# Preparing the right operands of a seven-product scheme earlier, value tiles by pairs of heads, and five pairs of input tiles instead of four

## The chip, the cores and the metric

The kernel runs on one core of a Trainium2 chip. The metric is the device time of one execution in microseconds (us). Less is better. Before the change three runs gave 1080.13, 1081.16 and 1081.58 us, a median of 1081.16 us.

## What is computed

One decoder layer over 1024 positions of width 1024, in float32. The part that the change touches is the first half of the layer, the mixer:

```
u = rms_norm(x, norm1_g)
z = u @ w_in                      # 1024 x 3584 columns
cb, cc, ch = three groups of 512 columns (convolution)
rq, rk, rv, rg = four groups of 512 columns (retention, 4 heads of 128)
y_conv = group_rms_norm(cb * causal_dwconv3(cc * ch))
q, k   = rotary(rq), rotary(rk);  v = rv
o      = chunkwise_retention(q, k, v)      # per head, 8 chunks of 128 rows
y_ret  = group_rms_norm(o) * silu(rg)
x = x + concat(y_conv, y_ret) @ w_out
```

Behind it stand an MLP with a squared ReLU (1024 to 4096 to 1024) and a last norm. The change doesn't touch those.

## The kernel before, in words

**Matrix products.** Everything is held transposed, channels on the partitions. Each float32 operand is split in two parts of a shorter format, hi and lo, and a product is taken as hi by hi, hi by lo and lo by hi. `split_piece` (L166) makes the two parts of a weight piece: `wh` by a copy on ACT, `wl = r - wh` by a subtraction on DVE, or on POOL where the planner's clock for POOL stands low enough. The input has the parts `uh` and `ul` for each of eight groups of 128 channels. The matmuls (all on L401, in `mm`) are 128x128 weights by 128x512 columns.

**A whole tile** is 128 columns of `z` for all 1024 positions. `tile_in` (L518) makes it in four quarters, two banks of PSUM at a time: 8 channel groups x 2 halves of positions x 3 products = 48 matmuls. `whole(f)` (L741) then takes it out of PSUM and starts the elementwise work of that tile, as convolution input or as gate.

**A pair** (`pair_in`, L821) makes two tiles of `z` at once with seven products of half the size in place of eight, in the manner of Strassen and Winograd: 7 products x 4 channel groups x 3 = 84 matmuls where two whole tiles take 96. Three of the seven have parts of `uh` and `ul` as their right operands, 36 matmuls; the other four need sums and differences of the input, called t1 to t4, 48 matmuls. These right operands are the tiles `U` (a hi and a lo part in one tile of 1024 columns). The generator `rights(j)` (L782) makes them for channel group j = 0 to 3: two DMAs that load the input anew into tiles `xs`, two scalings on ACT, four subtractions on DVE or POOL, then for each of t1 to t4 a copy on ACT (hi) and a subtraction on DVE or POOL (lo). Its first line waits for the end of a retention: `rights(0)` and `rights(1)` for that of the first, `rights(2)` and `rights(3)` for that of the second. Each pair also needs sums of weight pieces (`r<-r,r`, three per pair, on POOL) and sums of its products on DVE (`z<-z,b`, line 74).

**Retention.** `retention(p, q, k)` (L577) works on two heads, p = 0 or 1, in ten steps, one chunk of 128 positions after another: scores and transposes on PE, masks, states and tiny scale factors on DVE (`h<-b,bk,causal`, `S<-S,b`, and `m`, two columns wide), scaled copies on ACT. Its last PE instructions are the transposes on L661. The values are computed before it (L350 to L363) into four tiles `v` of 1024 columns, each with two chunks of all four heads.

**What sets the order of the work.** The program is written out by a planner in Python: `Task`s (generators) yield what they wait for, and `tick` and `background` put their next operations among the matmuls when the planner's own clocks of the engines say so. A group of 12 matmuls is one slot, 2.72 us on that clock. `IN_TURNS` (L40) is the order of the tiles after the four query and key tiles: a number is a whole tile, a bracket a pair. Before: whole tiles 0, 1, 2, 3 and 20, then the pairs (4,5), (6,7), (8,9) and (10,11), then 21; then come 22 and 23 (`IN_END`). Retention 1 runs among the first whole tiles. Tiles in SBUF of 128 x 1024 come from one pool, `big`, of 40 buffers. All elementwise operations are issued by one helper, so they have line 74 in the profile; they are told apart by the names of their tiles. After the mixer come the out-projection (L938 and on) and the MLP, L401 and L1274 by turns.

Of the kernel before, what the change touches and what calls it, by code (L numbers as in the profile page):

```python
# [16 lines left out]
P = 128  # L17
D = 1024
T = 1024
H = 512  # L20
# [16 lines left out]


IN_QK = [12, 13, 16, 17, 14, 15, 18, 19]
IN_TURNS = [0, 1, 2, 3, 20, (4, 5), (6, 7), (8, 9), (10, 11), 21]  # L40
IN_END = [22, 23]
SLOT, LOOK, PE_MARGIN, LATE = 2.72, 3.2, 1.2, 0.0
WARM = 10
# [36 lines left out]
def hybrid_layer(  # L80
# [41 lines left out]
    def unit(dt=F32, s="u"):  # L122
        return big.tile([P, T], dt, tag="u", name=nm(s))
# [217 lines left out]

    v = [unit(s="v") for _ in range(NC_ // 2)]
    rtok = cp.tile([P, NC_], F32, name="rtok")
    ms = xp.tile([P, NC_], F32, name="ms")
    r2 = xp.tile([P, NC_], F32, name="r2")
# [12 lines left out]
                        stop=(k == KT - 1 and a is ul),  # L360
                    )
    for c in range(NC_):
        act.copy(v[c // 2][:, hs[c % 2]], vb[c])  # L363

    def token_norms():
        b = bank(pr)
# [210 lines left out]
    def retention(p, q, k):  # L577
# [7 lines left out]
        for c in range(NC_ + 2):  # L585
            yield STEP_MARGIN
            now[0] += 1.7
            new = None
            if c < NC_:
                sl = slice(c * P, (c + 1) * P)  # L590
                bs = bank(pr)
                for j in range(2):
                    nc.tensor.matmul(bs[:, js[j]], k[j][:, sl], q[j][:, sl], start=True, stop=True)
                kz = None
                if c < NC_ - 1:
                    bt = bs[:, 2 * P :]
# [14 lines left out]
                new = (c, sc, kz)  # L611
                retention_task[p].ready = clock[dve]
            done, pend = pend, new
            turned, turn = turn, None
            if done is not None:
                pc, sc, kz = done
                psl = slice(pc * P, (pc + 1) * P)
                vt = v[pc // 2]
                v0 = (pc % 2) * H + h0 * P
                vj = [vt[:, v0 + j * P : v0 + (j + 1) * P] for j in range(2)]  # L620
                bo = bank(pr)
                for j in range(2):
                    nc.tensor.matmul(bo[:, js[j]], sc[:, js[j]], vj[j], start=True, stop=(S is None))
                    if S is not None:
                        nc.tensor.matmul(
                            bo[:, js[j]], q[j][:, psl], S[:, js[j]], start=False, stop=True
                        )
                if kz is not None:
                    bk = bo[:, 2 * P :]
                    for j in range(2):  # L630
                        nc.tensor.matmul(bk[:, js[j]], kz[:, js[j]], vj[j], start=True, stop=True)
# [24 lines left out]
                turn = (pc, on)  # L656
            if turned is not None:
                pc, on = turned
                b = bank(pr)
                for j in range(2):  # L660
                    nc.tensor.transpose(b[:, js[j]], on[:, js[j]], ident)  # L661
                for j in range(2):
                    act.copy(o[j][:, pc * P : (pc + 1) * P], b[:, js[j]])
                    if pc % 4 == 3:
                        o_n[h0 + j, pc // 4] = o[j]
                        mark(("o", h0 + j, pc // 4), act)
            if c >= NC_ - 1:
                retention_task[p].ready = clock[act]
            if c == NC_:
                mark(("retention", p), act)  # L670


# [78 lines left out]

        tile_in(evac)

    for p in range(2):
        q = rot_tiles(*ropes)
        if p == 0:
            rows_ = norm_rows()
        k = rot_tiles(*ropes)
        tick()
        spawn(retention(p, q, k), max(clock[dve], clock[pool]))  # L760
        retention_task[p] = procs[-1]
        del q, k


    U = {}

    def put_hi(name, j, src):
# [5 lines left out]
        hi, lo = U[name][j]  # L773
        eng.tensor_sub(lo, src, f32(hi))

    def product(n, bank_):
        name = {1: "11", 2: "21", 3: "22", 4: "t4", 5: "t1", 6: "t2", 7: "t3"}[n]
        b = bank(bank_)
        mm(parts.pop(0), [b], lambda _, k: U[name][k], True, True)
        return b  # L780

    def rights(j):  # L782

        yield "retention", j // 2
        if j % 2:
            yield "t4", j - 1
        a, b = (unit(s="xs") for _ in range(2))
        lo_, hi_ = hs
        for k, t in ((j, a), (4 + j, b)):
# [10 lines left out]
        eng.tensor_sub(b[:, hi_], b[:, hi_], a[:, lo_])  # L800
        eng = yield (pool, dve)
        eng.tensor_sub(b[:, lo_], b[:, lo_], b[:, hi_])
        for name, src in (("t1", a[:, lo_]), ("t2", b[:, hi_]), ("t3", a[:, hi_]), ("t4", b[:, lo_])):
            yield (act,)
            put_hi(name, j, src)
# [2 lines left out]
            mark((name, j), eng)  # L808

    rights_task = []  # L810
    for j in range(4):
        rights_task.append(Task(rights(j), now[0]))
        rights_task[j].go()
    spread_norms(rows_)
    for j in range(4):
        for c, name in ((0, "11"), (1, "21"), (2, "22")):
# [707 lines left out]
```

## Time and profile before

| | |
|---|---|
| three runs | 1080.13, 1081.16, 1081.58 us |
| the profiled execution, its time | 1082.14 us |
| the same, the span of its instructions | 1080.3 us |
| mean granted clock of TensorE | 0.995 |

Engines: PE is TensorE's matmuls, PEld its weight loads, DVE is VectorE, ACT ScalarE, POOL GpSimd, SP SyncE, whose queue issues the transfers. A row of the timeline has the start in us, the duration, engine, line, operation, the tiles it writes and reads, and in square brackets how long the engine stood idle before it and who released it. A row of a window table has the window, its length, the engine's busy time with its number of instructions (those cut by the ends count too), the granted clock as a share of full speed, then the share of the DMA engines and their GB/s. Matmuls overlap in the pipeline, so the duration of one is longer than the distance to the next.

### The profile page before, as it was taken

How to read it: one execution, taken by the hardware profiler on the slowest of the kernel's cores; microseconds unless marked ns; L12 is line 12 of the kernel's file. 1: busy time of each engine (PE TensorE's matmuls, PEld its weight loads, DVE VectorE, ACT ScalarE, POOL GpSimd, SP SyncE). 2: the span in 40 equal slices, each digit the busy share in tenths (PEclk: the TensorE clock that was granted, in tenths of full speed). 3: DMA queues.
4: the chain of work that ended last, by engine and by line, in shares of the span. 5: the costliest groups of instructions: out<-in, count | busy, mean ns of one | idle time of the engine just before them, and what ended most of it. 6: DMA issues, size and time to landing. Idle time of an engine off the chain costs nothing.

```text
span 1080.3 us, 14040 instructions
## 1 busy us (share of the span) xinstructions
PE 1060.6 (98%) x4936; PEld 882.7 (82%) x4936; DVE 881.2 (82%) x1255; ACT 463.3 (43%) x916; POOL 540.3 (50%) x370
## 2 busy tenths in 40 slices
PE   9999999999999999999999999999999999999996
PEld 7888888887778888788788888888888888888886
DVE  8446546799997666699999989999899899899945
ACT  8211445763335544444343443443343434334453
POOL 6233323256752132559548258267286295384543
PEclk9999999999999999999999999999999999999998
DMA  7121121212223635050121211211301211210204
GB/s 273 62 59 48 31 79 69 100 58 77 69 59 117 224 114 169 2 194 30 58 69 39 79 39 49 89 25 54 93 25 50 88 30 43 85 30 12 77 1 157
DMA packets 40311, 81.75 MB, mean 76 GB/s; under 512 B 4528, under 2 KB 6704, under 8 KB 40240
## 3 DMA queue, kind: packets, MB, share of 16 engines
q1 hardware_dynamic: 40240, 80.85, 23.2%
q8 instruction: 39, 0.64, 0.2%
q14 instruction: 32, 0.26, 0.1%
HBM read 71.40 MB, written 9.44 MB: 75 GB/s over the span
## 4 chain that ended last, share of the span: by engine, by line
PE 80%; DVE 11%; issue 3%; POOL 3%; ACT 2%; DMA 1%; POOLq 0%; DVEq 0%; SPq 0%; ACTq 0%
PE b L401 50%; PE b L1274 23%; PE b L355 4%; DVE z L74 2%; DVE wl L74 2%; POOL r L74 1%; POOL z L74 1%; DVE t L74 1%; DVE x L74 1%; DVE xs L74 1%; DVE U L74 1%; DVE q L74 1%; ACT h L74 1%; PE b L337 1%; DVE m L74 1%
## 5 line engine op out<-in xcount | busy, mean ns | idle before, releaser
L401 PE MATMUL b<-U,wh 128*128 128x512 f32 x1024 | 315.9, 390 | 2.4 <-DVE x L74 1.2
L74 ACT CAST wh<-r 128x512 fp32r<-128x512 f32 x286 | 175.9, 620 | 321.2 <-PE b L401 134.7
L74 DVE TENSOR_TENSOR wl<-r,wh 128x512 fp32r<-128x512 f32 x251 | 233.3, 932 | 90.9 <-ACT wh L74 90.0
L74 POOL TENSOR_TENSOR r<-r,r 128x512 f32<-128x512 f32 x136 | 209.8, 1545 | 116.0 <-DVE wl L74 65.6
L1274 PE MATMUL b<-V,wh 128*128 128x512 f32 x784 | 242.0, 389 | 0.7 <-POOL V L74 0.4
L401 PEld LDWEIGHTS b<-U,wh 128*128 128x128 f32 x1024 | 191.8, 188 | 43.4 <-issue 2.8
L74 DVE TENSOR_TENSOR x<-x,b 128x512 f32<-128x512 f32 (+1 forms) x320 | 197.8, 663 | 24.4 <-PE b L401 19.3
L401 PE MATMUL b<-U,wl 128*128 128x512 f32 x512 | 199.4, 389 | 0.0
L1274 PEld LDWEIGHTS b<-V,wh 128*128 128x128 f32 x784 | 147.0, 188 | 32.3 <-POOL V L74 0.8
L74 POOL TENSOR_TENSOR t<-t,t 128x512 f32<-128x512 f32 x70 | 106.3, 1523 | 97.9 <-ACT t L74 51.9
L1274 PE MATMUL b<-V,wl 128*128 128x512 f32 x392 | 152.5, 389 | 0.0
L74 POOL TENSOR_TENSOR wl<-r,wh 128x512 fp32r<-128x512 f32 x35 | 49.1, 1408 | 159.2 <-ACT wh L74 151.9
L401 PEld LDWEIGHTS b<-U,wl 128*128 128x128 f32 x512 | 96.0, 188 | 20.7 <-POOL wl L74 0.4
L401 PE MATMUL b<-uh,wh 128*128 128x512 f32 x304 | 103.3, 399 | 2.3 <-DVE z L74 2.3
L401 PE MATMUL b<-uh,wl 128*128 128x512 f32 x304 | 100.8, 392 | 1.1 <-DVE wl L74 1.1
L401 PE MATMUL b<-ul,wh 128*128 128x512 f32 x304 | 101.0, 392 | 0.0
L1274 PEld LDWEIGHTS b<-V,wl 128*128 128x128 f32 x392 | 73.6, 188 | 15.2
L74 POOL TENSOR_TENSOR V<-t,V 128x512 fp32r<-128x512 f32 x35 | 49.6, 1417 | 67.2 <-ACT V L74 67.2
L74 DVE TENSOR_TENSOR t<-t,b 128x512 f32<-128x512 f32 x112 | 75.8, 677 | 1.7 <-POOL t L74 1.2
L74 ACT ACTIVATE t<-t 128x512 f32<-128x512 f32 x64 | 40.2, 631 | 81.9 <-DVE t L74 81.3
L74 DVE TENSOR_TENSOR V<-t,V 128x512 fp32r<-128x512 f32 x63 | 70.3, 1116 | 0.0
L401 PEld LDWEIGHTS b<-uh,wl 128*128 128x128 f32 x304 | 57.3, 189 | 13.9 <-DVE wl L74 1.5
(168 smaller groups left out, 1431.0 us busy)
## 6 DMA issues: line engine op xcount, KB each, us to landing
r<-w_up_t SPq DMA_DIRECT2D x64, 256.0 KB, 2.6
r<-w_down_t SPq DMA_DIRECT2D x56, 256.0 KB, 2.7
r<-w_in_t SPq DMA_DIRECT2D x48, 256.0 KB, 2.6
xt<-xT SPq DMA_DIRECT2D x16, 256.0 KB, 5.4
xs<-xT SPq DMA_DIRECT2D x8, 512.0 KB, 4.8
r<-w_out_t SPq DMA_DIRECT2D x16, 256.0 KB, 2.7
x<-xT SPq DMA_DIRECT2D x8, 512.0 KB, 7.4
k<-x SPq DMA_DIRECT2D x6, 512.0 KB, 3.2
```

The lines of the kernel that those rows point to most:

```text
L74: return f(out, *args, **kw)
L337: nc.tensor.matmul(b[:, c * P : (c + 1) * P], d, ident, start=True, stop=True)
L355: nc.tensor.matmul(vb[i], a[k][:, i * P : (i + 1) * P], b[k // 2][:, vs], start=(k == 0 and a is uh and b is vh), stop=(k == KT - 1 and a ...
L401: nc.tensor.matmul(b, a[:, k, :], rhs(n, k)[r], start=(start and i == 0), stop=(stop and i == len(ops) - 1),)
L1274: nc.tensor.matmul(b, a, r, start=(i == 0), stop=(i == len(ops) - 1))
```

## The change

The values are kept by pairs of heads: `v[p, i]` holds four chunks of the two heads of retention p. The copies out of PSUM are 16 of 128x256, half on ACT and half on DVE, in place of 8 of 128x512 on ACT, and the two tiles of p are given back when retention p ends. `rights(j)` no longer waits for whole retentions at its start: its loads and first four subtractions go as soon as the first queries and keys are there (j = 0), or t4 of j = 0 (j = 1), the second queries and keys (j = 2), or t4 of j = 2 (j = 3); the waits for retention 0, t4 of j = 1 and retention 1 stand ahead of the second part of j = 1, 2 and 3. The order of the tiles is 20, 0, 1, then five pairs from (2,3) to (10,11), then 21. The order of the weight transfers follows `IN_TURNS`.

```
-IN_TURNS = [0, 1, 2, 3, 20, (4, 5), (6, 7), (8, 9), (10, 11), 21]
+IN_TURNS = [20, 0, 1, (2, 3), (4, 5), (6, 7), (8, 9), (10, 11), 21]
...
-    v = [unit(s="v") for _ in range(NC_ // 2)]
+    v = {(p, i): unit(s="v") for p in range(2) for i in range(2)}
...
     for c in range(NC_):
-        act.copy(v[c // 2][:, hs[c % 2]], vb[c])
+        for p, eng in ((0, act.copy), (1, dve.tensor_copy)):
+            to = slice(c % 4 * 2 * P, (c % 4 + 1) * 2 * P)
+            eng(v[p, c // 4][:, to], vb[c][:, p * 2 * P : (p + 1) * 2 * P])
...
             if c == NC_:
+                for i in range(2):
+                    del v[p, i]
                 mark(("retention", p), act)
...
     def rights(j):
-        yield "retention", j // 2
-        if j % 2:
-            yield "t4", j - 1
+        yield [("qk", 0), ("t4", 0), ("qk", 1), ("t4", 2)][j]
         a, b = (unit(s="xs") for _ in range(2))
...
         eng.tensor_sub(b[:, lo_], b[:, lo_], b[:, hi_])
+        if j:
+            yield [("retention", 0), ("t4", 1), ("retention", 1)][j - 1]
         for name, src in (("t1", a[:, lo_]), ("t2", b[:, hi_]), ("t3", a[:, hi_]), ("t4", b[:, lo_])):
...
+        mark(("qk", p), dve)
+        if p == 0:
+            for j in range(4):
+                rights_task.append(Task(rights(j), now[0]))
+                rights_task[j].go()
```

The whole program has 12 matmuls of 128x512 fewer on PE: those with `U` as the right operand go from 1024 to 1056 (`wh`) and from 512 to 528 (`wl`), the three kinds with `uh` or `ul` from 304 to 284 each. DVE has 14 instructions more, POOL 8 more (four sums of weight pieces and five splits `wl` more, one other less), ACT 3 more, SP as many as before.

Three places show how the order moves. The first is PE at the end of retention 1, whose last transposes are the row with L661; before:

```order
L401 MATMUL b_1803<-uh_164,wl_1529 128x512
L661 MATMUL b_1983<-ident,h_1934 128x128 x2
L401 MATMUL b_2004<-uh_157,wh_1641 128x512
L401 MATMUL b_2005<-uh_157,wh_1641 128x512
L401 MATMUL b_2004<-ul_165,wh_1641 128x512
L401 MATMUL b_2005<-ul_165,wh_1641 128x512
L401 MATMUL b_2004<-uh_157,wl_1642 128x512
```

After, where the line numbers are two higher:

```order
L403 MATMUL b_1858<-uh_164,wl_1581 128x512
L663 MATMUL b_2023<-ident,h_1980 128x128 x2
L403 MATMUL b_2047<-uh_157,wh_1694 128x512
L403 MATMUL b_2047<-ul_165,wh_1694 128x512
L403 MATMUL b_2047<-uh_157,wl_1695 128x512
L403 MATMUL b_2047<-uh_158,wh_1694 128x512
L403 MATMUL b_2047<-ul_166,wh_1694 128x512
```

Before, a whole tile follows (two banks by turns, b_2004 and b_2005), and one more after it, and then the first pair; after, the first product of the first pair (one bank) follows at once. The transposes are the 872nd row of PE's order in both.

The second place is DVE within retention 0. `m` are the tiny scale factors, `h` the masked scores, `S` the state; before:

```order
L74 SCALAR_TENSOR_TENSOR m_998<-m_998 128x2
L74 SCALAR_TENSOR_TENSOR h_1033<-b_1028,bk,causal 128x128 x2
L74 SCALAR_TENSOR_TENSOR S_1046<-S_990,b_1039 128x128 x2
L74 SCALAR_TENSOR_TENSOR m_1050<-m_1050,bq 128x2
L74 TENSOR_TENSOR m_1054<-m_1054 128x2
L74 SCALAR_TENSOR_TENSOR m_1054<-m_1054,m_1050 128x2
L74 SCALAR_TENSOR_TENSOR m_1054<-m_1054 128x2
L74 SCALAR_TENSOR_TENSOR h_1083<-b_1078,bk,causal 128x128 x2
```

After:

```order
L74 SCALAR_TENSOR_TENSOR m_966<-m_966 128x2
L74 TENSOR_TENSOR U_993<-xs_872,U_993 128x512
L74 TENSOR_TENSOR U_996<-xs_871,U_996 128x512
L74 SCALAR_TENSOR_TENSOR h_1022<-b_1017,bk,causal 128x128 x2
L74 SCALAR_TENSOR_TENSOR S_1035<-S_959,b_1028 128x128 x2
L74 SCALAR_TENSOR_TENSOR m_1039<-m_1039,bq 128x2
L74 TENSOR_TENSOR m_1043<-m_1043 128x2
L74 SCALAR_TENSOR_TENSOR m_1043<-m_1043,m_1039 128x2
L74 SCALAR_TENSOR_TENSOR m_1043<-m_1043 128x2
L74 TENSOR_TENSOR U_1055<-xs_872,U_1055 128x512
```

The lo parts of right operands (`U<-xs,U`) now stand between the chunk steps of retention 0.

The third place is DVE towards the end of the pair (4,5), which is the first pair before and the second after. `wl` is the lo part of a weight piece, `z` and `cv` are sums of products and convolution values; before:

```order
L74 TENSOR_TENSOR wl_2350<-r_2189,wh_2349 128x512
L74 TENSOR_TENSOR z_2200<-z_2200,b_2336 128x512
L74 SCALAR_TENSOR_TENSOR cv_2250<-a_2095,sm,cv_2250 128x512 x2
L74 TENSOR_TENSOR wl_2376<-r_2218,wh_2375 128x512
L74 TENSOR_TENSOR z_2200<-z_2200,cv_2250 128x512
L74 TENSOR_TENSOR wl_2402<-r_2245,wh_2401 128x512
L74 TENSOR_TENSOR z_2360<-z_2361,b_2388 128x512
```

After:

```order
L74 TENSOR_TENSOR wl_2371<-r_2210,wh_2370 128x512
L74 TENSOR_TENSOR z_2216<-z_2216,b_2357 128x512
L74 SCALAR_TENSOR_TENSOR cv_2259<-z_2046,sm,cv_2259 128x512 x2
L74 TENSOR_TENSOR wl_2396<-r_2234,wh_2395 128x512
L74 TENSOR_TENSOR z_2216<-z_2216,cv_2259 128x512 x2
L74 TENSOR_TENSOR z_2380<-z_2381,b_2409 128x512
```

Of two neighbours one has changed: the last split `wl` of the piece stands on POOL after the change, and a product `z<-z,cv` on DVE that stood on POOL. From `z_2360` (before) and `z_2380` (after) to the end of the program DVE has the same 957 rows in both, and PE, ACT and POOL have the same rows too, from 240.8, 270.5 and 268.2 us of the profile of before on.

More of the change, by code (lines that the diff above doesn't have):

```diff
@@ L617, in retention @@
                 psl = slice(pc * P, (pc + 1) * P)
-                vt = v[pc // 2]
-                v0 = (pc % 2) * H + h0 * P
+                vt = v[p, pc // 4]
+                v0 = pc % 4 * 2 * P
                 vj = [vt[:, v0 + j * P : v0 + (j + 1) * P] for j in range(2)]
@@ L752, in whole @@
         tile_in(evac)
[L754 to L762, printed above, removed]
     U = {}
@@ L774, in put_lo @@
         eng.tensor_sub(lo, src, f32(hi))
[L776 to L780, printed above, removed]
     def rights(j):
-        yield "retention", j // 2
-        if j % 2:
-            yield "t4", j - 1
+        yield [("qk", 0), ("t4", 0), ("qk", 1), ("t4", 2)][j]
         a, b = (unit(s="xs") for _ in range(2))
@@ L810, in hybrid_layer, with product @@
     rights_task = []
-    for j in range(4):
-        rights_task.append(Task(rights(j), now[0]))
-        rights_task[j].go()
+    for p in range(2):
+        q = rot_tiles(*ropes)
+        if p == 0:
+            rows_ = norm_rows()
+        k = rot_tiles(*ropes)
+        tick()
+        spawn(retention(p, q, k), max(clock[dve], clock[pool]))
+        retention_task[p] = procs[-1]
+        del q, k
+        mark(("qk", p), dve)
+        if p == 0:
+            for j in range(4):
+                rights_task.append(Task(rights(j), now[0]))
+                rights_task[j].go()
+    def product(n, bank_):
+        name = {1: "11", 2: "21", 3: "22", 4: "t4", 5: "t1", 6: "t2", 7: "t3"}[n]
+        b = bank(bank_)
+        mm(parts.pop(0), [b], lambda _, k: U[name][k], True, True)
+        return b
     spread_norms(rows_)
```

## The prediction

> **What bounds the kernel now.** I read the page first, then PE's waits in the stretch from 210 to 330 us, then the windows of that stretch, and last DVE's timeline there. The shares and the slices of the page:
>
> ```profile
> PE 1060.6 (98%) x4936; PEld 882.7 (82%) x4936; DVE 881.2 (82%) x1255; ACT 463.3 (43%) x916; POOL 540.3 (50%) x370
> ...
> DVE  8446546799997666699999989999899899899945
> ```
>
> PE is busy 98% of the span, so a removed matmul should count in full, unless PE then waits. DVE's slices (27 us each) are at nine tenths from the eighth to the eleventh, about 190 to 300 us: there the pairs of input tiles run. How the two stages differ:
>
> ```profile
> 100.00:210.00 110.00, 108.80 (x634) 94.39 (x633) 68.42 (x171) 54.76 (x201) 33.22 (x25) 1.00 0.18 61
> 210.00:320.00 110.00, 104.88 (x450) 84.19 (x450) 104.27 (x111) 52.83 (x89) 66.85 (x43) 0.99 0.23 75
> ```
>
> The columns behind the length are PE, PEld, DVE, ACT, POOL. From 100 to 210 us (queries, keys, retentions, first whole tiles) PE is idle 1.2 us and DVE is busy 62%. From 210 to 320 us PE is idle 5.1 us and DVE is busy 95%. PE's waits in that second stretch, and three of them on the timeline:
>
> ```profile
> PE b L401 <- DVE z L74: 2.3, 1, 2.3
> PE b L401 <- DVE wl L74: 1.1, 1, 1.1
> PE b L481 <- ACT s L74: 1.0, 1, 1.0
> PE b L482 <- DVE s L74: 0.4, 2, 0.2
> PE b L482 <- DVE r L74: 0.3, 1, 0.3
> 264.82 0.50 PE L401 MATMUL b<-uh,wl 128*128 128x512 f32 x1 [1.12 <-DVE wl L74]
> 268.65 0.50 PE L482 MATMUL b<-s,blkr 128*128 128x512 f32 x1 [0.22 <-DVE s L74]
> 318.60 0.80 PE L401 MATMUL b<-uh,wh 128*128 128x512 f32 x1 [2.27 <-DVE z L74]
> ```
>
> They add up to the idle time, and nearly all of it is DVE's doing. So in the pair stage two engines are close to being the bound: PE leads, catches up with DVE and waits. The change takes matmuls from PE and adds work to DVE in just this stage, and the wait at 264.82 us decides what it is worth.
>
> After the longest wait the clock falls:
>
> ```profile
> 319.00:320.00 1.00, 1.00 (x3) 0.50 0.00 0
> 321.00:322.00 1.00, 1.00 (x4) 0.57 0.00 0
> 322.00:323.00 1.00, 1.00 (x6) 1.00 0.00 0
> 318.60 12.48 PE b L401 x47
> 331.98 108.81 PE b L401 x480
> ```
>
> The next to last number of a window's main columns is the granted clock (0.50, 0.57, 1.00). The last two rows are of the chain: 480 matmuls take 108.81 us where PE runs freely, 0.2267 us each; the 47 behind the wait take 12.48 us in place of 10.65, so the slow clock cost 1.8 us.
>
> **The change part by part.** *Matmuls.* 12 fewer x 0.2267 = 2.72 us. Both orders reach the end of retention 1 at the same row of PE, at 209.8 us of before:
>
> ```profile
> 209.79 0.52 PE L661 MATMUL b<-ident,h 128*128 128x128 f32 x2
> 210.07 0.71 PE L401 MATMUL b<-uh,wh 128*128 128x512 f32 x2
> ```
>
> From there PE alone would come to the matmul that waits for `wl` 2.72 us sooner: it stood ready at 264.82 - 1.12 = 263.70 us, and would at 260.98 us.
>
> *DVE and POOL from there to that split.* Before, the first pair began when the two whole tiles behind retention 1 were through, and DVE issued 26 instructions from its first row of that pair (at 238.13 us) to the split's end at 264.77 us. After, two pairs lie between retention 1 and the same split, and in the order I count 50 DVE instructions from the first row of pair (2,3) through the split, beside 21 on POOL. Prices from the same stage:
>
> ```profile
> 238.13:264.77 26.64, 24.30 (x28) 1.00 0.24 70
> 212.59:264.70 52.11, 49.36 (x52) 1.00 0.24 81
> 264.80:323.70 58.90, 55.19 (x60) 0.97 0.22 67
> 212.59:264.70 52.11, 32.47 (x21) 1.00 0.24 81
> 263.01 1.76 DVE L74 TENSOR_TENSOR wl<-r,wh 128x512 fp32r<-128x512 f32 x1
> ```
>
> The first three are DVE's windows (each counts two that its ends cut), the fourth is POOL's for the second. The last pair-sized piece costs 26.64 / 26 = 1.025 us per DVE instruction, gaps included; the 50 whole ones from 212.59 us cost 52.11 / 50 = 1.042, and those also run beside 21 POOL instructions; the next 60, up to the long wait, cost 58.90 / 60 = 0.982. When can DVE begin?
>
> ```profile
> 210.80 0.69 DVE L74 TENSOR_TENSOR U<-xs,U 128x512 fp32r<-128x512 f32 x1
> 211.41 1.28 DVE L74 TENSOR_TENSOR z<-b,R 128x512 f32<-128x512 f32 x2
> ```
>
> At the end of retention 1 DVE is not behind: it takes a whole tile's product out of PSUM at 211.41 us, directly after PE has finished it. I let the pair's work begin at 211.7 us, an estimate from these two rows. Then the split is done at 211.7 + 50 x 1.025 = 262.95 us, against 264.77 us: 1.8 us sooner. PE, ready at 260.98 us, waits 2.0 us in place of 1.12 us and goes on 0.05 us behind the split as before, at 263.0 us, 1.8 us sooner. At 0.982 it is done at 260.8 us, PE doesn't wait and is 3.84 us ahead there; at 1.042, at 263.8 us, 1.0 us ahead. It would be no gain at 1.061. I take 1.025, because that row has the kinds of instruction that the second of the new pairs has, and no subtractions for the right operands.
>
> *After that.* From there to the end all engines have the same rows. The waits of 1.00, 0.22, 0.27 and 2.27 us are between instructions of that common part, and the DVE lag that ends in the wait at 318.60 us builds up again from 264.80 us on, where DVE has been waited out. So they come again, and the shift stays -1.8 us to the end.
>
> *Right operands made early.* The loads of `xs`, 8 of 512 KB, now stand on SP's queue inside retention 0 and 1, with weight pieces behind them.
>
> ```profile
> xs<-xT SPq DMA_DIRECT2D x8, 512.0 KB, 4.8
> 194.75 0.97 DVE L74 TENSOR_TENSOR m<-m 128x2 f32<-128x2 f32 x1 [0.27 <-ACT m L74]
> 195.76 1.19 DVE L74 SCALAR_TENSOR_TENSOR m<-m,m 128x2 f32<-128x2 f32 x1
> 196.98 0.16 DVE L74 SCALAR_TENSOR_TENSOR m<-m 128x2 f32<-128x2 f32 x1
> 197.86 0.44 PE L661 MATMUL b<-ident,h 128*128 128x128 f32 x2 [0.63 <-ACT h L74]
> PE b L661 <- ACT h L74: 1.2, 3, 0.6
> 194.10:197.10 3.00, 2.83 (x3) 1.00 0.53 171
> ```
>
> They land in 4.8 us, and the stores of `o` that share the queue wait for ACT's copies at the end of retention 1; the weight piece behind them is needed about 9 us later. DVE has 41.6 us free in 100 to 210 us, and takes over at most 16 of the 32 subtractions there, at 1 us each. So PE sees none of it in the sum. The cost that could show is in the chain of a chunk step: the tiny `m` operations take 0.97 and 1.19 us here, the like in 0.16 us just behind, while POOL is at work (the last row is its window), and PE waited 0.63 us behind them. Retention now has more POOL work beside it. PE's waits of this kind are three, 1.2 us in all, so I bound the change between -1 us (the step moves away from POOL's work) and +2 us (three or four more of 0.6). I take zero. The t1 of j = 3 is needed at the third product, 210.07 + 2 x 2.72 = 215.5 us; the order has its last subtractions ahead of the evacuation of the second product. This also stays at zero, with the same +2 as its bound.
>
> *Values.* 16 copies of 128x256 on two engines for 8 of 128x512 on ACT.
>
> ```profile
> L74 ACT COPY v<-b 128x512 f32<-128x512 f32 x8 | 4.1, 601 | 19.5 <-PE b L355 19.5
> 52.83 1.37 DVE L74 TENSOR_TENSOR wl<-r,wh 128x512 fp32r<-128x512 f32 x1 [15.01 <-ACT wh L74]
> ```
>
> DVE had stood idle for 15.01 us up to 52.83 us, so its eight cost nothing; if they held its next split up, that would be below 1 us, and the halves on ACT save about as much. Zero.
>
> The sum: -1.8 us on the profiled execution, whose span is 1080.3 us and whose own time is 1082.14 us; it lies 0.98 us above the median of 1081.16 us. So 1078.5 us of span, 1080.3 us of time, and against the median 1081.16 - 1.8 = **1079.4 us**. About 0.2%, 2.16 us, is what a measurement of this kernel can tell from none, so the line for faster is 1079.0 us: the forecast lies just on the side of no difference.
>
> **The rivals.** *PE is the bound throughout.* DVE works at 0.982 or less and the wait at 264.82 us goes, with the 0.22 us behind it: -2.72 - 1.12 - 0.22 = -4.1 us, 1077.1 us. For it: in the new stage no `xs` subtractions are left, and these fall among the dearest rows. Against it: the 26.64 us piece had hardly any either. It may go further: the half clock came after a gap of 2.27 us and not after 1.12 or 1.00, so a somewhat shorter wait at 318 us, if DVE comes there less late, spares 1.8 us more: -5.9 us, 1075.3 us. The Trainium skill, "TensorE: Matmul & The Clock Gate", section "Part 1: The HAM clock gate", says that the clock is halved after an idle window of about 3.4 us, counted in windows that run on by themselves; a gap of 2.27 us should by that rule not do it, and here it did. Chance 0.27.
>
> *DVE is slowed by POOL and becomes the bound.* Where they work side by side DVE is dearer:
>
> ```profile
> 226.25:237.50 11.25, 11.03 (x10) 1.00 0.00 0
> L74 DVE TENSOR_TENSOR wl<-r,wh 128x512 fp32r<-128x512 f32 x5 | 6.5, 1295 | 0.1
> L74 DVE TENSOR_TENSOR z<-z,b 128x512 f32<-128x512 f32 x9 | 6.1, 680 | 0.1
> ```
>
> The window is 1.125 us per instruction. The groups (278 to 302 us) show why: a subtraction with both inputs in SBUF takes 1295 ns, one with an input in PSUM 680 ns, and the one at 263.01 us took 1.76 us. If pairs (2,3) and (4,5) run at 1.125 throughout, the split is done at 211.7 + 56.3 = 268.0 us, 3.2 us later than before, PE waits 7 us, and the clock falls once more for about 1.8 us: +3.2 to +5, 1084.4 to 1086.2 us. It decides from 1.061 us per instruction on and exceeds 0.2% at 1.105. For it: two pairs in a row, 21 POOL instructions. Against it: 50 instructions beside as many on POOL cost 1.042. The Trainium skill, "SBUF — State Buffer", section "Who interferes with whom", says that a DVE instruction with two SBUF inputs and a GpSimd instruction that reads SBUF lock each other out whole. By it each of 21 POOL instructions could hold DVE up for its full length, 32.47 / 21 = 1.5 us, and 50 x 0.69 + 21 x 1.5 = 66 us would end the split at 277.7 us, 13 us late; the longest subtraction here, 1.76 us, is less than 0.69 + 1.5, so the trace bears out part of it. Chance 0.15.
>
> *The operands are not there early after all.* Retention steps or t1 hold PE up by the +2 us above: -1.8 + 2 = about zero, 1081.4 us. The rows of `m` speak for it; the 41.6 us free on DVE against it. Chance 0.13.
>
> **How the numbers follow.** The forecast has 0.45. Between its ends, -1.0 and -2.7 us, the third beyond -2.16 us, 0.15, lies below 1079.0 us and 0.30 above. The first rival adds 0.26 to faster and 0.01 to no difference, the second 0.14 to slower and 0.01 to none, the third 0.12 to none and 0.01 to slower. That is 0.41 faster, 0.44 the same, 0.15 slower. The range goes from the first rival's lower end, 1075.3 us, to the third's bound without the gain, 1081.16 + 2 = 1083.2 us.
>
> **What would show it.** In the profile of the changed kernel the counterpart of the wait at 264.82 us stands near 263.0 us with about 2.0 us for `wl`; DVE from the end of retention 1 to it takes near 51 us for 50 instructions; the wait of 2.3 us for `z` and the clock of 0.50 come again near 316.8 us; PE's waits ahead of 210 us stay near 1.2 us. No wait there, or no slow clock, is the first rival; a wait of several us the second; new waits for `h` on L663 or for `U` at the third product the third. The forecast is wrong if the last transposes of retention 1 don't come near 209.8 us, or if waits of the common part change their size.

## The result, and the profile after

The changed kernel takes 1092.37 us (1092.33 to 1092.81), the kernel before beside it 1081.34 us: a ratio of 1.0108, interval 1.0093 to 1.0122. It is 11 us slower, where 1079.4 us was forecast. The profiled execution has a span of 1090.5 us.

The page of the changed kernel, engines and DVE's slices:

```profile
PE 1060.0 (97%) x4924; PEld 880.8 (81%) x4924; DVE 890.3 (82%) x1269; ACT 462.0 (42%) x918; POOL 550.0 (50%) x378
...
DVE  7546657589998656689999989989899899899945
```

DVE looks nearly as before. PE is idle for 30.5 us of its span (1090.5 - 1060.0) in place of 19.7 us (1080.3 - 1060.6). PE's waits say where. All of them from 50 to 340 us:

```profile
PE b L663 <- ACT h L74: 9.2, 9, 2.1
PE b L625 <- ACT h L74: 3.6, 3, 1.6
PE b L403 <- DVE z L74: 2.3, 1, 2.3
PE b L483 <- ACT s L74: 1.0, 1, 1.0
PE b L484 <- DVE s L74: 0.4, 2, 0.2
PE b L403 <- DVE wl L74: 0.3, 1, 0.3
PE b L484 <- DVE r L74: 0.3, 1, 0.3
```

The two places of the prediction on its timeline:

```profile
223.46 0.59 PE L663 MATMUL b<-ident,h 128*128 128x128 f32 x2 [0.47 <-ACT h L74]
274.85 0.50 PE L403 MATMUL b<-uh,wl 128*128 128x512 f32 x1 [0.29 <-DVE wl L74]
```

The first row was 1.2 us before (L661), the second is new: 12.8 us in place of 1.2, all in the chunk steps of the retentions. Retention 1 ends at 223.46 us in place of 209.79, 13.67 us later, after the same number of matmuls. 11.6 us of this are these waits; the other 2 us are PE's busy time, which from 100 us to there rose from 108.6 to 110.5 us. The wait for `wl` is at 274.85 us in place of 264.82, 10.03 us later. So the pairs did gain: 13.67 - 10.03 = 3.64 us, which is 2.8 us of PE's own way there (263.70 - 209.79 = 53.91 us before, 274.56 - 223.46 = 51.10 us after) and 0.83 us of the wait. Behind it the shift is 10.2 us up to the wait for `z` and 8.7 us behind that wait, because the slow clock of the kernel before doesn't come; PE then waits more near 512 and 516 us (0.23 and 1.09 us in place of 0 and 0.48), and the span's shift is 10.2 us again.

DVE's window from the first row of the pair stage to that wait:

```profile
225.00:274.80 49.80, 46.94 (x52) 1.00 0.25 80
```

The window holds 50 whole instructions, 1.0 us each. The wait for `z` came again with its size, and these are PE's windows behind it:

```profile
328.82 0.50 PE L403 MATMUL b<-uh,wh 128*128 128x512 f32 x1 [2.27 <-DVE z L74]
```

```profile
329.00:330.00 1.00, 1.00 (x5) 1.00 0.00 0
330.00:331.00 1.00, 1.00 (x6) 1.00 0.00 0
```

The granted clock stayed at 1.00 this time.

**One chunk step that waits.** All engines from 117 to 123 us in retention 0, without the input tile's matmuls:

```profile
117.11 1.66 ACT L74 CAST U<-xs 128x512 fp32r<-128x512 f32 x3
117.81 1.29 POOL L74 TENSOR_TENSOR U<-xs,U 128x512 fp32r<-128x512 f32 x1 [6.12 <-ACT U L74]
118.29 3.07 DVE L74 TENSOR_TENSOR U<-xs,U 128x512 fp32r<-128x512 f32 x2 [1.72 <-ACT U L74]
...
119.37 1.44 POOL L74 TENSOR_TENSOR wl<-r,wh 128x512 fp32r<-128x512 f32 x1 [0.26 <-ACT wh L74]
...
121.28 0.60 DVE L74 SCALAR_TENSOR_TENSOR h<-b,bk,causal 128x128 f32<-128x128 f32 x2
...
121.97 0.63 ACT L74 ACTIVATE h<-b,bz 128x128 f32<-128x128 f32 x2 [2.67 <-DVE h L74]
...
122.65 0.49 PE L625 MATMUL b<-v,h 128*128 128x128 f32 x2 [1.62 <-ACT h L74]
```

The scores that `h<-b,bk,causal` masks here were in PSUM 6.9 us before 121.28 us (PE made them from 113.77 us on, by counting scores and masks). But two lo parts stand ahead of the mask in DVE's queue. DVE first idles 1.72 us for ACT's copies, then needs 3.07 us for the two, beside POOL. Only then come mask, ACT's scaled copy, and PE, 1.62 us late. Counted so for all 16 chunks, the masks start on average 1.8 us behind their scores before and 4.2 us after. The groups of the two retentions (105 to 225 us) show the same over all steps, first before, then after:

```profile
L74 DVE TENSOR_TENSOR U<-xs,U 128x512 fp32r<-128x512 f32 x11 | 10.0, 933 | 4.4 <-ACT U L74 4.3
L74 DVE SCALAR_TENSOR_TENSOR h<-b,bk,causal 128x128 f32<-128x128 f32 x32 | 9.7, 342 | 3.3 <-PE b L598 3.2
```

```profile
L74 DVE TENSOR_TENSOR U<-xs,U 128x512 fp32r<-128x512 f32 x12 | 9.9, 838 | 11.5 <-ACT U L74 11.5
L74 DVE SCALAR_TENSOR_TENSOR h<-b,bk,causal 128x128 f32<-128x128 f32 x32 | 9.6, 342 | 0.3 <-PE b L595 0.3
```

The last numbers are DVE's idle time ahead of the group and who ended it. Before, DVE waited 3.2 us for PE ahead of the masks: it was early. After, it is never early (0.3 us), yet it idles 11.5 us ahead of the lo parts.

### The profile page after: what moved, and what is told of

It is laid out like the page before. It is cut to its first block, busy times and chain, and to the rows that moved or that the text cites. A ratio compares the mean times of both kernels' runs of the same rounds, so it can differ in the third digit from the quotient of the medians.

```text
span 1090.5 us, 14042 instructions
## 1 busy us (share of the span) xinstructions
PE 1060.0 (97%) x4924; PEld 880.8 (81%) x4924; DVE 890.3 (82%) x1269; ACT 462.0 (42%) x918; POOL 550.0 (50%) x378
## 4 chain that ended last, share of the span: by engine, by line
PE 71%; DVE 16%; ACT 5%; issue 4%; POOL 3%; DMA 1%; POOLq 0%; DVEq 0%; ACTq 0%; SPq 0%
PE b L403 43%; PE b L1280 22%; PE b L355 4%; DVE z L74 3%; DVE wl L74 2%; ACT h L74 2%; DVE q L74 2%; DVE t L74 1%; DVE m L74 1%; DVE U L74 1%; DVE x L74 1%; POOL r L74 1%; DVE cv L74 1%; DMA x<-k 1%; DVE xs L74 1%
## 5 line engine op out<-in xcount | busy, mean ns | idle before, releaser
L403 PE MATMUL b<-U,wh 128*128 128x512 f32 x1056 | 325.8, 390 | 3.0 <-DVE x L74 1.1
L74 POOL TENSOR_TENSOR r<-r,r 128x512 f32<-128x512 f32 x140 | 214.4, 1533 | 116.2 <-DVE wl L74 66.9
L403 PEld LDWEIGHTS b<-U,wh 128*128 128x128 f32 x1056 | 197.8, 188 | 45.3 <-issue 1.9
L403 PE MATMUL b<-U,wl 128*128 128x512 f32 x528 | 205.6, 389 | 0.0
L74 POOL TENSOR_TENSOR wl<-r,wh 128x512 fp32r<-128x512 f32 x40 | 56.2, 1413 | 158.7 <-ACT wh L74 154.5
L403 PEld LDWEIGHTS b<-U,wl 128*128 128x128 f32 x528 | 99.1, 188 | 21.1 <-DVE wl L74 0.4
L403 PE MATMUL b<-uh,wh 128*128 128x512 f32 x284 | 97.2, 397 | 2.3 <-DVE z L74 2.3
L403 PE MATMUL b<-uh,wl 128*128 128x512 f32 x284 | 95.2, 390 | 0.3 <-DVE wl L74 0.3
L403 PE MATMUL b<-ul,wh 128*128 128x512 f32 x284 | 95.2, 390 | 0.0
L403 PEld LDWEIGHTS b<-uh,wl 128*128 128x128 f32 x284 | 53.3, 188 | 12.1 <-DVE wl L74 0.7
```

Of the source, the lines that this page charges most:

```text
L74: return f(out, *args, **kw)
L403: nc.tensor.matmul(b, a[:, k, :], rhs(n, k)[r], start=(start and i == 0), stop=(stop and i == len(ops) - 1),)
```

## The experiments

Theory A: the early work on right operands stands among the small operations of the chunk steps and delays them. Theory B: the new order of the tiles does, with the gate among the steps. Theory C: the values' new place does. In the text "end" is the start of retention 1's last transposes, 209.79 us before and 223.46 us after; times are set against the kernel before of the same session (1080.05 to 1080.81 us; the changed kernel is +11.0 us against its own).

**1. Five pairs, right operands as late as before.** In the changed kernel:

```
-        yield [("qk", 0), ("t4", 0), ("qk", 1), ("t4", 2)][j]
+        yield "retention", j // 2
+        if j % 2:
+            yield "t4", j - 1
...
-        if j:
-            yield [("retention", 0), ("t4", 1), ("retention", 1)][j - 1]
```

> The changed kernel, with the waits of the right operands as they were before (j = 0 and 1 start after retention 0, j = 2 and 3 after retention 1); five pairs, the new order of the tiles and the values by pairs of heads stay. Theory A (the early right operands stand in the queues of DVE and ACT ahead of the small operations of the chunk steps, so PE waits for h): retention 1 ends at 211 to 215 us in place of 223.5, PE's waits for h fall from 12.8 us to 2 to 5 us (what is left is the gate's table loads, some 2.4 us, and POOL beside the m operations); but the first pair then waits for t1 to t4 of j = 2 and 3, 15 to 30 us in all, so the whole is slower than the changed kernel, 1095 to 1110 us. Theory B (the new order of the tiles, with the gate's tile among the retention's steps and no whole tile behind it, makes the waits): they stay at 10 us or more and retention 1 ends at 221 us or later.

Measured: 1097.9 us, +17.3. The end is 214.57 us. Its longest waits:

```profile
PE b L403 <- ACT U L74: 7.2, 1, 7.2
PE b L663 <- ACT h L74: 5.4, 7, 1.3
PE b L403 <- POOL U L74: 2.6, 1, 2.6
PE b L403 <- DVE U L74: 1.4, 1, 1.4
```

The waits for h fall nearly as A says, and the first pair waits for its operands, 11.2 us, less than expected; the granted clock was then at half for 14 us. Five pairs do need the operands earlier. Of B some 5 us stay.

**2. Four pairs, right operands early; 3. the gate third; 4. the values alone.**

```
-IN_TURNS = [20, 0, 1, (2, 3), (4, 5), (6, 7), (8, 9), (10, 11), 21]
+IN_TURNS = [0, 1, 2, 3, 20, (4, 5), (6, 7), (8, 9), (10, 11), 21]     # run 2
+IN_TURNS = [0, 1, 20, (2, 3), (4, 5), (6, 7), (8, 9), (10, 11), 21]   # run 3
```

> The changed kernel with the old order of the tiles (0, 1, 2, 3, 20, four pairs); the right operands early and the values by pairs of heads stay. Theory A: PE's waits for h are 6 to 11 us, retention 1 ends 5 to 10 us later than the 209.8 us of before, and the whole is 1085 to 1090 us, as the first pair has its operands ready and loses less. Theory B: waits for h of 1 to 2 us as before, 1080 to 1081 us.

> The changed kernel with the gate's tile third in place of first (0, 1, 20, then the five pairs). Theory A with the gate as a second cause: the two table loads at 185.5 and 190.0 us leave the chunk steps of retention 1, the waits of 0.71 and 1.67 us behind them go, and the whole is 2 to 3 us faster, 1089 to 1090.5 us; the waits in retention 0 stay at about 6.2 us. If the gate has no part in it: 1092 us and the same waits. Theory B expects most of the 10 us to go, 1082 to 1085 us.

Run 4 is the kernel before with the three changes to `v` and nothing else.

> The kernel before with only the values kept by pairs of heads (16 copies of 128x256 on ACT and DVE in place of 8 of 128x512 on ACT). Theories A and B both: no difference, 1080.5 to 1082 us, PE's waits for h at 1 to 2 us. Theory C (the other place of the values disturbs the retention steps): waits for h of several us and 1084 us or more.

Measured: run 2, 1085.25 us, +4.6, end 217.27 us with 8.0 us of waits for h. Run 3, 1084.86 us, +4.2, end 218.83 us, 9.4 us; this time lies in the range of Theory B and not of A. Run 4, 1080.31 us, ratio 0.9998 (0.9989 to 1.0008), end 209.51 us. Theory C falls. The early right operands alone make 7.5 us at the end of retention 1 (run 2), and the fifth pair 1.6 us more (run 3). The gate's place adds more than the two table loads that I had in mind: +11.0 us in place of +4.2, of which 4.6 us come before the end of retention 1 and 2.9 us in the pairs up to 305 us, where the wait of 1.0 us for `s` went. Whether the gate does this by itself is the question of run 5.

**5. No work on right operands.** Each ACT, DVE and POOL operation in `rights` is replaced by the advance of the planner's clock, the copies within `put_hi`:

```
     def put_hi(name, j, src):
-        u = unit(F32R, "U")
-        act.copy(u[:, :H], src)
-        U.setdefault(name, [None] * 4)[j] = (u[:, :H], u[:, H:])
+        pass_time(act, H)
+        U.setdefault(name, [None] * 4)[j] = (uh[j][:, :H], ul[j][:, :H])
...
-            act.activation(t, t, AF.Copy, scale=sm[:, G1 + k : G1 + k + 1])
+            pass_time(act, T)
...
-        eng.tensor_sub(a[:, lo_], a[:, hi_], a[:, lo_])
+        pass_time(eng, H)
```

> The changed kernel without the arithmetic of the right operands: t1 to t4 are not made (parts of the input stand in their place in the products), while their loads stay, the planner's clocks are moved on as if the work were done, and the rest keeps its order. Theory A (that work delays the chunk steps, worth some 8 us): retention 1 ends at 212 to 216 us in place of 223.5, PE waits 2 to 6 us for h in place of 12.8, and the whole is 1081.5 to 1086 us. Theory B (the new order of the tiles alone makes the waits): retention 1 ends at 221 us or later and the whole is 1090 us or more.

Measured: 1072.37 us, -8.2, end 208.54 us, lower than any theory had it. Its waits for h and the masks' row:

```profile
PE b L663 <- ACT h L74: 0.8, 2, 0.5
```

```profile
L74 DVE SCALAR_TENSOR_TENSOR h<-b,bk,causal 128x128 f32<-128x128 f32 x32 | 9.7, 344 | 8.2 <-PE b L600 6.9 <-PE b L595 1.2
```

The gate's tile is still first here, and PE hardly waits; DVE idles 8.2 us for PE ahead of the masks. Its two table loads stand in retention 1 as well (174.6 and 179.1 us). So the whole 14.9 us at the end of retention 1 (223.46 - 208.54) hang on the right operands' work, and the gate does harm only beside it. Theory B as a cause by itself falls. The time of 1072.37 us is not the price of that work alone: the stage behind the mixer also calls `put_hi`, so 16 copies on ACT (`U<-un`, from 387 us on in the changed kernel) are left out there too. Just ahead of those PE is 7.7 us ahead of the kernel before, at the end of the span 9.0 us.

**6. The gate's table loads; 7. a shorter queue; 8. the square on ACT.** Run 6 and run 8 change one line each, run 7 the planner's look ahead for these tasks (`RIGHTS_LOOK` is 1.6, where `look` is 3.2):

```
-        act.activation(g[:, sl], g[:, sl], AF.Silu)
+        act.activation(g[:, sl], g[:, sl], AF.Silu if h else AF.Copy)
...
-                        if start < now[0] + look:
+                        if start < now[0] + (min(look, RIGHTS_LOOK) if task in rights_task and look < 1e6 else look):
...
-        dve.tensor_mul(t, r, r)
+        act.activation(t, r, AF.Square)
```

> The changed kernel with a plain copy in place of the Silu of the first gate tile (20), so that the two table loads of ACT at 185.5 and 190.0 us fall away; nothing else moves on any engine. If the loads make the gate's part of the loss: the waits of 0.71 and 1.67 us behind them go, 2 to 3.5 us in all, 1089 to 1090.5 us. If the gate's part comes from its other work (its DVE and POOL operations, or the place of the other tiles): less than 1 us, 1091.5 us or more.

> The changed kernel, but the planner may put work of the right operands on an engine only where that engine's clock stands less than 1.6 us ahead of PE's, in place of 3.2 us. All the work stays, on PE in the same order. Theory A, as a matter of order in the queues: fewer of these operations stand ahead of the masks and the m operations, the waits on the matmuls with v (3.6 us) halve, and the whole is 2 to 5 us faster, 1087 to 1090.5 us. If it is the amount of work and not its place: 1092 us as before.

> The changed kernel with r*r of the tiny scale factors as a square on ACT, in place of a DVE product of two inputs (mean 388 ns in the changed kernel's retentions, 211 ns in the kernel before, 1.07 us beside POOL work). If POOL's hold on DVE makes part of the waits: 16 x 0.2 us off the chains, 1 to 3 us faster, 1089.5 to 1091.5 us. If not: 1092 us, or slower where ACT is the late engine.

Measured: run 6, 1090.26 us, +9.7, end 220.75 us: beside the right operands' work the two loads cost 2.7 us there, as expected. Run 8, 1088.63 us, +8.1, end 219.78 us: 3.7 us, a little more than expected. By the expectation that speaks for POOL's hold as a part, but the run also takes 16 operations out of DVE's queue. Run 7, 1104.9 us, a miss in the whole: the end is 213.91 us, 9.5 us earlier, but the work put off from the retentions came back in the first pair, where the granted clock was also at half twice for 10 us. Its longest waits from 50 to 340 us (line numbers are one higher; the second row is of the retentions):

```profile
PE b L484 <- ACT s L75: 8.6, 1, 8.6
PE b L664 <- ACT h L75: 4.2, 5, 1.7
PE b L404 <- DVE U L75: 3.6, 2, 2.2
PE b L404 <- ACT U L75: 2.7, 2, 2.2
```

**9. No scalings; 10. no differences.** Only these operations of run 5 are left out.

> The changed kernel without the scalings of the input tiles on ACT (8 of 128x1024, 1.17 us each); the operands are then made from unscaled input, and all else keeps its place. Theory A says that all the work on right operands, 15 us of delay in retention 1's end by the run without it, stands in the queues of ACT, DVE and POOL: if ACT's share counts, retention 1 ends 2 to 5 us earlier than 223.5 us and the whole is 1087.5 to 1090.5 us. If only DVE and POOL count: 1091.5 to 1092.5 us.

> The changed kernel without the four differences per channel group (16 of 128x512 on DVE and POOL); the operands are then copies of scaled input, and all else keeps its place. If DVE's and POOL's share counts: retention 1 ends 3 to 6 us earlier, 1086.5 to 1089.5 us. If only ACT counts: 1091.5 to 1092.5 us.

Measured: run 9, 1086.09 us, +5.9, end 218.26 us; run 10, 1080.81 us, +0.6, end 214.40 us. Both are further down than expected. Leaving out 8 ACT operations is worth 5.2 us and leaving out 16 on DVE and POOL 9.1 us at the end of retention 1. Both profiles even have 3.4 us of half clock in retention 1 (from 205.0 and 202.0 us), and the changed kernel's has none there. The two need not add up, and no run leaves out the copies and lo parts alone; what is the operations' own time and what is waiting between them isn't told apart.

**11. All on DVE; 12. all on POOL; 13. all on DVE in the version of run 14.** In `rights`:

```
-        eng = yield (pool, dve)
+        eng = yield (dve,)     # runs 11 and 13;  (pool,) in run 12
```

> The changed kernel with all differences and lo parts of the right operands on DVE, none on POOL. If they delay the chunk steps by standing ahead of the masks and m operations in DVE's queue, more stand there: retention 1 ends later than 223.5 us, 1092.5 to 1096 us. If it is POOL's work that makes the two-input operations on DVE slow (m of 1.07 us in place of 0.16): fewer of these, retention 1 ends 2 to 5 us earlier, 1087.5 to 1090.5 us.

> The changed kernel with all differences and lo parts of the right operands on POOL, none on DVE. Queue of DVE as the cause: DVE has only its own small operations left, the waits on the matmuls with v go, retention 1 ends 3 to 6 us earlier; POOL's hold on DVE as the cause: m operations of about 1.1 us become the rule, the waits of L663 grow from 9.2 us, and retention 1 ends later. If the operands come late for the first pair, PE waits for U there, and the whole is slower by that wait, so the end of retention 1 decides and not the time.

> The kernel with two right operands made from the first queries on, with all their differences and lo parts on DVE. Queue of DVE as the cause: slower than 1079.75 us by 1 to 3 us. POOL's hold as the cause: 1 to 3 us faster, 1077 to 1079 us.

Measured: run 11, 1091.68 us, +10.9, end 223.35 us; run 12, 1095.21 us, +14.4, end 228.97 us; run 13, 1084.31 us, +3.5, where run 14 has -0.4, end 219.06 us in place of 213.27. POOL's hold is seen on the `m` operations of the changed kernel, as a group from 105 to 225 us and in one step on the timeline, there by sums of weight pieces:

```profile
L74 DVE TENSOR_TENSOR m<-m 128x2 f32<-128x2 f32 x16 | 6.2, 388 | 6.5 <-ACT m L74 6.5
```

```profile
205.43 3.96 POOL L74 TENSOR_TENSOR r<-r,r 128x512 f32<-128x512 f32 x3
...
206.99 1.07 DVE L74 TENSOR_TENSOR m<-m 128x2 f32<-128x2 f32 x1 [0.27 <-ACT m L74]
...
208.10 0.16 DVE L74 SCALAR_TENSOR_TENSOR m<-m,m 128x2 f32<-128x2 f32 x1
208.30 1.11 DVE L74 SCALAR_TENSOR_TENSOR m<-m 128x2 f32<-128x2 f32 x1
```

In run 11 the group's mean is 217 ns in place of 388, so that hold is gone, and the end is the same. But its profile has the granted clock at half twice in the retentions, for 3.4 us behind waits of 2.60 and 2.13 us, which the changed kernel's has not. The second of them:

```profile
210.11 0.44 PE L663 MATMUL b<-ident,h 128*128 128x128 f32 x2 [2.13 <-ACT h L74]
211.00:212.00 1.00, 1.00 (x4) 0.50 0.00 0
```

By the matmuls that ran slowly this cost some 3.3 us (an estimate), and the mean granted clock of all four measured executions is 0.992 to 0.993 in place of 0.995 to 0.996. So run 11 doesn't show that taking the hold off is worth nothing; more work in DVE's queue and less hold may also outweigh each other in it. In run 12 DVE has none of the work, and the waits are the longest of all:

```profile
PE b L663 <- ACT h L74: 11.3, 8, 4.0
PE b L625 <- ACT h L74: 3.3, 2, 2.0
```

Some 3.4 us of its later end are half clock again (an estimate, from two stretches in the retentions). The end moved as POOL's hold would have it, but not by way of `m`: the mean of `m<-m` is 222 ns, while DVE's idle time ahead of `m<-m,bq`, waiting for ACT's `h`, rose from 15.6 to 20.0 us. Run 13 went the way of DVE's queue, and by more than expected. So the three runs don't name one engine: each moves both things at once. What runs 11 and 12 share is that the work is one chain over ACT and another engine, queued among the steps; that this is what counts fits both runs, but they don't show it.

**14. Two operands first; 15. the same with the square; 16. copies first; 17. both.** Run 14 starts j = 0 and 1 ahead of the first queries, with the gate third; run 15 also makes the differences of j = 2 later; run 16 changes the end of `rights` in the changed kernel; run 17 is run 14 with that:

```
-        yield [("qk", 0), ("t4", 0), ("qk", 1), ("t4", 2)][j]
+        yield [0.0, 0.0, ("qk", 1), ("t4", 2)][j]
...
-        if j:
-            yield [("retention", 0), ("t4", 1), ("retention", 1)][j - 1]
+        if j > 1:
+            yield [("t4", 1), ("retention", 1)][j - 2]
...
-        for name, src in (("t1", a[:, lo_]), ("t2", b[:, hi_]), ("t3", a[:, hi_]), ("t4", b[:, lo_])):
+        ts = (("t1", a[:, lo_]), ("t2", b[:, hi_]), ("t3", a[:, hi_]), ("t4", b[:, lo_]))
+        for name, src in ts:
             yield (act,)
             put_hi(name, j, src)
+        for name, src in ts:
             eng = yield (pool, dve)
             put_lo(name, j, src, eng)
```

> The kernel with the gate's tile third, and with the right operands of j = 0 and 1 made from the first queries on, so largely ahead of retention 0, where DVE and ACT have idle time; j = 2 as after the second queries, j = 3 after that. All the work is there. Theory A: retention 0 loses its waits, 5 to 6 us, against the kernel with the gate third (1084.9 us): 1078 to 1081 us. If the work costs the same wherever it stands: 1084 to 1085 us.

> The same, with r*r of the tiny scale factors as a square on ACT, and the differences of j = 2 directly after t4 of j = 1. Theory A with POOL's hold on DVE as a part: 1 to 3 us less than the kernel with two operands first, 1076 to 1080 us, below both kernels. If the square brings nothing here: the same as that kernel.

> The changed kernel with the hi copies of t1 to t4 of a channel group all ahead of their lo parts, so that a lo part on DVE need not wait for the copy on ACT just before it. The amount of work is the same. In the changed kernel DVE stands idle 11.5 us in the retentions ahead of these lo parts, waiting for ACT, with the masks h behind them in its queue. If that standing in the queue is the cause: this idle time falls to under 5 us, retention 1 ends 3 to 7 us earlier than 223.5 us, 1085.5 to 1089.5 us. If the amount of work on ACT is: four copies in a row stand ahead of the small ACT operations, no gain or a loss, 1092 to 1094 us.

> The same order of copies and lo parts in the version with two right operands made from the first queries on and the gate third (1079.75 us). Standing in the queue as the cause: 1 to 3 us faster, 1077 to 1079 us. Amount as the cause: no change or slower.

Measured: run 14, 1079.75 us, ratio 0.9989 (0.9979 to 0.9998), end 213.27 us: the same work in the idle stretch ahead of retention 0 costs some 5 us less than in run 3. Run 15, 1079.47 us, end 216.29 us, no difference to run 14 in time that the runs can tell. Run 16, 1088.56 us, +8.5 in place of +11.0, end 220.49 us. Run 17, **1077.93 us**, ratio 0.9984 (0.9975 to 0.9994), end 214.29 us. Run 16's lo parts, then run 17's lo parts and masks:

```profile
L74 DVE TENSOR_TENSOR U<-xs,U 128x512 fp32r<-128x512 f32 x13 | 11.5, 928 | 1.2 <-ACT U L74 1.2
```

```profile
L74 DVE TENSOR_TENSOR U<-xs,U 128x512 fp32r<-128x512 f32 x12 | 10.4, 904 | 0.9 <-ACT U L74 0.9
L74 DVE SCALAR_TENSOR_TENSOR h<-b,bk,causal 128x128 f32<-128x128 f32 x32 | 9.7, 344 | 4.3 <-PE b L600 3.9 <-PE b L595 0.4
```

In run 16 the idle time ahead of the lo parts fell from 11.5 to 1.2 us, and retention 1 ended 3.0 us earlier, although ACT loads tables four times in place of two there (187.9 to 197.5 us). So the order of issue is shown to be a part. That the standing in the queue for another engine is what does it is not shown alone: DVE's idle time ahead of `m<-m,bq`, for ACT's `h`, rose from 15.6 to 23.1 us at the same time, and the mean of `m<-m` fell from 388 to 217 ns. Run 17 beats both kernels, the one before by 0.16% only. It doesn't tell whether the order of the copies helps there: its interval overlaps that of run 14, and its end is 1.0 us later, with one stretch of half clock ahead of it (from 110.1 us).

What goes with the end over all the runs is how late the masks come. The mean time from a chunk's scores to its masks, counted from the timelines:

| kernel | masks behind scores, us | end, us | half clock in the retentions |
|---|---|---|---|
| run 5, no right work | 1.7 | 208.54 | none |
| before | 1.8 | 209.79 | none |
| run 17 | 2.0 | 214.29 | once |
| run 1, rights late | 2.0 | 214.57 | none |
| run 14 | 2.6 | 213.27 | none |
| run 16 | 3.5 | 220.49 | none |
| run 2 | 3.7 | 217.27 | none |
| run 11 | 4.1 | 223.35 | twice |
| changed kernel | 4.2 | 223.46 | none |
| run 12 | 4.4 | 228.97 | twice |

The masks are late in run 12 too, where DVE's queue holds none of the work and waits for ACT instead. How much of the work stands among the steps, and where, counts besides (runs 3, 9, 10, 14). How much each of DVE, ACT and POOL adds in a single step stays open.

## Why the prediction was wrong

The step that failed is the one headed *Right operands made early*: "So PE sees none of it in the sum", with zero taken and +2 us as the bound. PE did see it: retention 1 ended 13.7 us later. 7.5 us of this come from the early right operands alone, under the old order of the tiles (run 2), 1.6 us with the fifth pair (run 3), and 4.6 us with the gate's tile among the steps, for which the prediction has no term at all. Without the arithmetic of the right operands all of it goes, 14.9 us (run 5). The working compared 41.6 us free on DVE from 100 to 210 us with 16 subtractions of 1 us, which asks whether the work fits, not whether the chunk step behind it in the queue comes late. In a chunk step the scores pass from PE over DVE's masks back to PE, the result from there over ACT, DVE, ACT, DVE and ACT to PE's transposes, and the next step follows after 12 matmuls; the row that told of it, 0.63 us of wait at 197.86 us, was read as a price of three such waits, not as a sign that the chain had no slack. One reading of the page was off as well, with no weight in the sum: the slices at nine tenths are DVE's ninth to twelfth, 216 to 324 us.

Point by point:

- *Matmuls*: right. 2.72 us forecast, 2.8 us measured from the end of retention 1 to the wait.
- *DVE in the new pairs*: the estimate of 1.025 us per instruction was high, 1.0 measured; PE's wait came out at 0.29 us and not 2.0 us, which is nearly the first rival's case. The stage gained 3.6 us where 1.8 was forecast.
- *After that*: right that the waits of the stage come again, the longest with the same 2.27 us. That the slow clock behind it didn't come in this execution is luck and gave 1.5 us; waits near 512 and 516 us, which the prediction held to be the same, grew and gave most of it back.
- *Values*: right, run 4 has a ratio of 0.9998.
- *The first rival* nearly held in its place, with 3.6 of its 4.1 us, and was outweighed more than three times by the third. Run 5, without the work on right operands, is 7.7 us ahead of the kernel before where its other omission begins, nearly twice the 4.1 us.
- *The second rival*, DVE slowed by POOL in the pairs: not there. POOL's hold does show in the retentions, on `m`; no run takes it off by itself, so its share of the delay stays open (runs 8, 11 and 12).
- *The third rival* named the right mechanism, new waits for `h` on L663, and gave it +2 us and a chance of 0.13. Its price was short by a factor of seven, or of nearly four by run 2 alone. The gate's table loads, 2.7 us by run 6 beside the right operands' work, are nowhere in the prediction: the gate was moved among the steps, and I had looked at its matmuls only.

The Trainium skill, "SBUF — State Buffer", section "Who interferes with whom", says that a DVE instruction with two SBUF inputs is held up whole by a GpSimd instruction that reads SBUF. The `m` rows agree: 0.16 us at 208.10 us, and 1.07 and 1.11 us for two that each end with one of the three POOL operations of 1.3 us. The prediction used this rule for the large subtractions in the pairs, where it decided nothing.

## What to carry to other kernels

Idle time of an engine is no cover for work put ahead of short dependent operations in its in-order queue; price such work by the latency of the chain behind it, and look at how late the chain's first operation comes behind its input (the masks 1.8 us before, 4.2 us after). The idle time ahead of that operation is the weaker sign: DVE waits 3.2 us for PE ahead of the masks before and 0.3 us after, but 3.3 us in run 11, which ends as late. Work that feeds a later stage is cheap where no such chain runs, here ahead of the first retention (run 14), and there may be something to gain by queueing its own steps so that none waits for the one just issued on another engine (3.0 us in run 16). A tile that is moved takes all its operations along, table loads too.

## What was not expected of the hardware

The same wait of 2.27 us for `z` was followed by half a clock for about 3.4 us in 9 of the 17 profiles that have it, the one before among them, and by none in 8, the one after among them; what decides it the runs don't tell. It is worth 1.8 us, the size of the gain that was forecast. Shorter waits were followed by it too, the shortest of 1.64 us in run 12, while one of 2.13 us in the changed kernel's retention 1 was not. The Trainium skill, "TensorE: Matmul & The Clock Gate", section "Part 1: The HAM clock gate", has windows that run on by themselves, which fits that the same wait does and doesn't trip it; its idle window of about 3.4 us is longer than the 2.27 us that did, and there the measurement decides.
